# The second half of an output projection in a fixed order on the matrix engine, with router products between the halves of its tiles

## The chip, the cores and the metric

The kernel runs on one core of a Trainium2 chip. The time is the device time of one execution, in microseconds (us). A core has five engines that work side by side, each through a program of its own in order, and wait for one another by semaphores: TensorE (PE; its weight loads are shown apart, as PEld), VectorE (DVE), ScalarE (ACT), GpSimd (POOL) and SyncE (SP). Here SP issues nearly all DMA transfers, in the order of its program; POOL issues the gathers and scatters by index.

## The reference, cut to what matters

The kernel computes one layer of a decoder for 512 prompt rows and 32 sample rows: attention and a state-space mixer, an output projection, and a mixture of 16 experts. The part that changes stands between the mixers and the experts:

```
mixed = concat([rmsnorm(att), y_ssm]) @ w_out        # 1024 x 1024
x = x + mods[2] * mixed
h = rmsnorm(x, g_norm2) * (1 + mods[4]) + mods[3]
lg = h @ w_rg + b_rg ;  le = h @ w_re + b_re         # router: 4 + 16 logits
# best of 4 groups, best 2 of its 4 experts, softmax weights
y = x + mods[5] * sum over the chosen experts of weight * expert(h)
```

An expert computes `silu(h @ w_gate) * (h @ w_up)` and multiplies it by `w_down`.

## The kernel before, in words

The 512 prompt rows are four tiles of 128 rows, t = 0 to 3; the 32 sample rows are a small fifth tile. The 1024 output columns of the projection are computed in two halves of 512. Each half sums over eight blocks k of 128 inputs, taken in the order 4 to 7, then 0 to 3 (`ko`). A float32 product is made of three reduced products, since weights and inputs are each split in a high and a low part: `catH` and `catL` hold the inputs, `wH` and `wL` the weights of the second half. A tile of the second half is thus 8 x 3 = 24 products of 128x512 into one accumulator `acc`.

Every tile then goes through these steps, each of them a function before:

- `first_half(t)`: ScalarE squares the first 512 columns of `x1` and sums them; TensorE turns (transposes) these columns in four pieces into a tile of PSUM, `evac` copies them to SBUF (`h2T`) on VectorE or ScalarE by a fixed pattern, and four small products with the folded router weights `wrP` give the first part of the 20 logits (`pr`), which VectorE copies to `lg`. GpSimd multiplies the first half of the normalised row, `h2`. Of `h2` there are two buffers, so tile t+2 needs that tile t has been written out.
- `mixed_tile(t)`: the 24 products; VectorE multiplies them by the gate and adds them to `x1`.
- `routed_tile(t)`: the same squares, turns and router products for the second 512 columns; on VectorE a reciprocal root by three Newton steps (`rsqrt_col`, single-column operations), the logits, the rest of `h2`, and `rank`, six small VectorE operations that end in `Ab`, the marks of the chosen experts. SP stores `x1` to the output `y_prompt` and `h2` to `h2d` in DRAM.
- `sample_rows()`: the like for the 32 sample rows (`h2S`, `lgS`).

`Ab` of all five tiles is counted on TensorE, VectorE works out each row's place (`posm`, `oh`, `gir`), and GpSimd gathers the first expert's rows from `h2d` (`xg`, L1921). It waits for the places and for all writes to `h2d`. The experts start with these rows.

The string `OSEQ` gives the order in which the steps are written down; a planner with costs and priorities sets each engine's order from it. The router steps are written at a higher priority (`high_priority(offset=100)`), `rank` at a lower one. SP also loads expert weights here. Weight tiles `gu` share a ring of seven buffers with `wL`: the second part of expert 2 and the first part of expert 3 go to the buffers of `wL` and are loaded once the last product with it is done. The weights `gux` of expert 4 go where the sample rows' tiles stood.

`in_turn` (which stands in the program and is used for an earlier projection) ties TensorE's instructions to the order in which they are written.

Of the kernel before, what the change touches and what calls it, by code (L numbers as in the profile page):

```python
# [29 lines left out]
OSEQ = 'm0 s f0 m1 r0 f1 m2 r1 f2 f3 m3 r2 r3'  # L30
# [20 lines left out]
def hybrid_step(ctx: ExitStack, tc: tile.TileContext, a, o):  # L51
# [1555 lines left out]
    def router(src, n, w, hf):  # L1607

        with tc.high_priority(offset=100):
            pt = PS()  # L1610
            for i in range(4):
                T.transpose(pt[:, n * i:n * i + n], src[:, (4 * hf + i) * P:(4 * hf + i + 1) * P], ident[0:n, 0:n])
            hT = W(p6, [P, 4, n], F32, "h2T", 3)
            evac(hT, pt[:, 0:4 * n].rearrange("p (k c) -> p k c", c=n))
            pr = PS("pr")
            for i in range(4):
                mm(pr[0:n, 0:20], hT[:, i, :], w[:, 4 * hf + i, :], start=i == 0, stop=i == 3)
            return pr[0:n, 0:20]
# [36 lines left out]
    def sample_rows():  # L1655
        h2 = W(p6s, [NS, D], F32, "h2S", 1)
        ss = W(p6, [NS, 1], F32, "ss2")
        S.activation(h2, xs1, AF.Square, accum_out=ss)
        x = W(p6, [NS, 1], F32, "ms2")
        V.tensor_scalar(x, ss, 1.0 / D, EPS, op0=OP.mult, op1=OP.add)  # L1660
        r = rsqrt_col(x, "h2s")
        V.scalar_tensor_tensor(h2, xs1, r, a2S, op0=OP.mult, op1=OP.mult)
        V.tensor_add(h2, h2, m3S)
        SP.dma_start(h2d[512:512 + NS, :], h2)
        lgS = lg[0:NS, 4, :]
        V.tensor_tensor(lgS, router(h2, NS, wr, 0), rb[0:NS], op=OP.add)
        V.tensor_tensor(lgS, router(h2, NS, wr, 1), lgS, op=OP.add)
        rank(4)
# [36 lines left out]
    def first_half(t):  # L1705

        ss = W(p6, [P, 1], F32, "ss2")
        square(x1[:, t, :], P, 0, ss)
        V.tensor_scalar(ms[:, t:t + 1], ss, 1.0 / D, EPS, op0=OP.mult, op1=OP.add)
        V.tensor_copy(lg[:, t, :], router(x1[:, t, :], P, wrP, 0))  # L1710
        h2s[t] = W(p6, [P, D], F32, "h2")
        G.tensor_mul(h2s[t][:, 0:512], x1[:, t, 0:512], M[:, 2, 0:512])

    def mixed_tile(t):

        acc = PS("acc")
        sl = slice(t * P, (t + 1) * P)
        for k in ko:
            mm(acc, catH[:, k, sl], wH[:, k, :], start=k == ko[0], stop=False)
            mm(acc, catH[:, k, sl], wL[k // 4][:, k % 4, :], start=False, stop=False)  # L1720
            mm(acc, catL[:, k, sl], wH[:, k, :], start=False, stop=k == ko[-1])
        tmp = W(p6, [P, 512], F32, "t512", 2)
        V.tensor_tensor(tmp, acc, M[:, 0, 512:D], op=OP.mult)
        V.tensor_add(x1[:, t, 512:D], x1[:, t, 512:D], tmp)

    def routed_tile(t):
# [5 lines left out]
        r = rsqrt_col(x, "h2")  # L1732
        V.tensor_tensor(lg[:, t, :], router(xr, P, wrP, 1), lg[:, t, :], op=OP.add)
# [15 lines left out]

    for step in OSEQ.split():  # L1750
        if step == "s":
            sample_rows()
            close_p6s()
            pw2["s"], close_pws = pool("pws", "right")
            early("s")
        else:
            (first_half if step[0] == "f" else mixed_tile if step[0] == "m" else routed_tile)(int(step[1]))
            if step == "m3":
                close_p6w()
                pw2["w"], close_pww = pool("pww", "right")  # L1760
                load_part(2, 2, 1)
                load_part(3, 3, 0)
                early("w")
# [374 lines left out]
    close_pws()  # L2138
# [37 lines left out]
```

## Time and profile before

| | us |
|---|---|
| median of 3 runs | 785.82 |
| the runs | 785.45, 785.82, 791.01 |
| the profiled execution, its own time | 787.62 |
| its span, first to last instruction | 785.9 |
| PE busy | 709.3 (90%) |
| DVE busy | 501.2 (64%) |
| ACT busy | 355.2 (45%) |
| POOL busy | 151.6 (19%) |

The mean granted TensorE clock of the profiled execution was 0.938 of full speed. The span is shorter than the time by 1.7 us, which lie around it. Busy shares are means over stages with different limits; the stage of the change is the stretch from 527 us, where the products of the second half start, to 572 us, where the first gather starts. In the profile TensorE's rows are pipelined: a product that starts every 0.23 us is shown with 0.39 us of its own.

### The profile page before, as it was taken

To read this page: it belongs to the slowest core of one execution; us is meant where nothing else is said; L and a number is where in the kernel's file an instruction comes from. 1 tells how busy PE (TensorE), PEld (TensorE's weight loads), DVE (VectorE), ACT (ScalarE), POOL (GpSimd) and SP (SyncE) were. 2 spreads that over 40 slices of the span, in tenths; PEclk is the share of its full clock that TensorE was granted. 3 is DMA by queue.
4 is the path that set the end of the run, shared out by engine and by line. 5 is a ranking of instruction groups with operands and counts; after the bars stand their busy time and mean duration, and the time that the engine had idled before them with its cause. 6 is when DMAs were issued, how large, how long until landed. Compare 5 with 4: busy or idle time off the path is not lost. (4 is left out here: it accounts for less than half of the span.)

```text
span 785.9 us, 14689 instructions
## 1 busy us (share of the span) xinstructions
PE 709.3 (90%) x5565; PEld 511.7 (65%) x5565; DVE 501.2 (64%) x1333; ACT 355.2 (45%) x813; POOL 151.6 (19%) x169
## 2 busy tenths in 40 slices
PE   4999999898999578998989999899668999999993
PEld 3667877676777355665647756687655766767562
DVE  5633692524644767554557555878986888877773
ACT  3423444515233333364434435613433766677661
POOL 1103012121321421010111200020131232233221
PEclk9999999889899879699999889999868999999997
DMA  8964895144559634423445041988767899997311
GB/s 286 355 187 131 289 330 193 58 162 161 214 191 346 253 143 172 149 81 134 164 158 219 2 108 23 360 267 286 290 253 282 270 333 335 334 329 256 86 25 23
DMA packets 67094, 161.86 MB, mean 206 GB/s; under 512 B 19005, under 2 KB 31238, under 8 KB 60622
## 3 DMA queue, kind: packets, MB, share of 16 engines
q1 hardware_dynamic: 56798, 115.54, 42.3%
q0 software_dynamic: 10224, 45.37, 17.5%
q8 instruction: 44, 0.72, 0.4%
q14 instruction: 28, 0.23, 0.1%
HBM read 153.48 MB, written 20.74 MB: 222 GB/s over the span
## 5 line engine op out<-in xcount | busy, mean ns | idle before, releaser
L92 PE MATMUL acc<-wh,hH 128*128 128x512 f32 (+1 forms) x128 | 48.9, 382 | 0.5 <-issue 0.5
L92 PE MATMUL acc<-wl,hH 128*128 128x512 f32 (+1 forms) x128 | 47.3, 370 | 0.0
L92 PE MATMUL acc<-wh,hL 128*128 128x512 f32 (+1 forms) x128 | 47.1, 368 | 0.0
L817 ACT ACTIVATE psb<-s,amx 128x128 f32<-128x128 f32 (+3 forms) x64 | 33.7, 528 | 27.4 <-DVE amx L815 24.3
L92 PE MATMUL acc<-gu,XF 128*128 128x512 f32 x88 | 46.1, 606 | 0.0
L92 PE MATMUL acc<-wh,XH 128*128 128x512 f32 x68 | 44.7, 657 | 0.4 <-ACT XH L1942 0.4
L815 DVE TENSOR_REDUCE amx<-s 128x1 f32<-128x128 f32 (+3 forms) x64 | 30.9, 484 | 17.3 <-PE s L92 17.3
L92 PE MATMUL ps<-wada,scT 128*32 128x128 f32 x768 | 38.0, 301 | 4.1 <-DMA wada<-in_w_ada 3.0
L92 PE MATMUL s<-KT,QT 128*128 128x384 f32 (+3 forms) x128 | 39.3, 392 | 1.3 <-DVE qa L838 0.8
L335 DVE TENSOR_TENSOR wl<-dn,wh 128x512 fp32r<-128x512 f32 x52 | 34.0, 686 | 7.0 <-ACT wh L334 6.9
L92 PEld LDWEIGHTS ps<-wada,scT 128*32 128x32 f32 x768 | 30.6, 122 | 10.3 <-issue 3.6
L1047 POOL DMA_INDIRECT gsel<-in_cache_sel,idx x16 | 20.6, 1289 | 84.3 <-PE smo L92 72.6
L334 ACT CAST wh<-dn 128x512 fp32r<-128x512 f32 x52 | 30.9, 619 | 12.9 <-PE acc L92 11.2
L820 PE MATMUL pt<-ident,psb 128*128 128x128 f32 x160 | 33.3, 308 | 3.3 <-ACT psb L817 3.3
L1991 POOL DMA_INDIRECT out_y_prompt<-yo,gi x13 | 21.4, 1646 | 74.8 <-DVE yo L1985 20.1
L335 DVE TENSOR_TENSOR wl<-gu,wh 128x512 fp32r<-128x512 f32 x44 | 29.5, 685 | 8.4 <-ACT wh L334 7.6
L92 PE MATMUL acc<-wh,HH 128*128 128x512 f32 x68 | 32.3, 478 | 1.6 <-ACT HH L1974 1.2
L334 ACT CAST wh<-gu 128x512 fp32r<-128x512 f32 x44 | 26.1, 619 | 15.8 <-PE acc L92 10.8
L92 PE MATMUL smo<-kt,Qb 128*32 128x512 f32 x80 | 29.6, 614 | 2.3 <-DVE kt L100 2.3
L102 ACT COPY kt<-sm 128x512 f32<-128x512 f32 x32 | 18.5, 584 | 27.6 <-PE sm L1023 24.0
L1985 DVE TENSOR_TENSOR yo<-acc,M 128x512 f32<-128x512 f32 x34 | 23.1, 686 | 11.5 <-PE acc L92 9.1
L92 PE MATMUL acc<-wl,HH 128*128 128x512 f32 x68 | 28.6, 421 | 0.0
(788 smaller groups left out, 1902.9 us busy)
## 6 DMA issues: line engine op xcount, KB each, us to landing
wada<-in_w_ada SPq DMA_DIRECT2D x24, 1024.0 KB
dn<-in_w_down SPq DMA_DIRECT2D x12, 1024.0 KB
gu<-in_w_gate SPq DMA_DIRECT2D x21, 512.0 KB
gu<-in_w_up SPq DMA_DIRECT2D x21, 512.0 KB
gux<-in_w_gate SPq DMA_DIRECT2D x11, 512.0 KB
gux<-in_w_up SPq DMA_DIRECT2D x11, 512.0 KB
wt<-in_cache_win SPq DMA_DIRECT2D x4, 1024.0 KB
wout<-in_w_out SPq DMA_DIRECT2D x4, 1024.0 KB
```

The lines of the kernel that those rows point to most:

```text
L92: T.matmul(out, lhsT, rhs, start=start, stop=stop)
L102: S.copy(out, in_)
L334: S.copy(wh[:, 0:n], w)
L335: (eng or V).tensor_sub(wl[:, 0:n], w, wh[:, 0:n].bitcast(F32))
L815: V.tensor_reduce(mx, ps[:, 0:n], axis=AX.X, op=OP.max, negate=True)
L817: S.activation(pb[:, 0:n], ps[:, 0:n], AF.Exp, bias=mx, accum_out=sm[:, h:h + 1])
L820: T.transpose(pt[:, c * P:(c + 1) * P], pb[:, c * P:(c + 1) * P], ident)
L1047: G.indirect_dma_start(out=t.rearrange("p r c -> p (r c)"), out_offset=None, in_=sel_rows, in_offset=bass.IndirectOffsetOnAxis(ap=idx[:, 2 ...
L1985: V.tensor_tensor(yo[:, cols], po, M5[:, cols], op=OP.mult)
L1991: G.indirect_dma_start(out=y_p, out_offset=bass.IndirectOffsetOnAxis(ap=gi, axis=0), in_=yo, in_offset=None, bounds_check=511, oob_is_err= ...
```

## The change

The order of the steps is written anew, finer, and TensorE's instructions are tied to it by `in_turn`, step by step:

- the 24 products of a tile are cut in two halves of 12 (`a`, k = 4 to 7, and `b`, k = 0 to 3);
- `first_half` and `routed_tile` are each cut in the turns (`F`, `R`) and the router products (`f`, `r`), as are the sample rows (`S`, `s`; before them stands `s` alone, the part without TensorE);
- between the halves, and between one tile and the next, stand turns and router products: those of the first columns of the same tile, and those of the second columns of the tile before;
- the loads of weights that need freed buffers (`load_part(2, 2, 1)`, `load_part(3, 3, 0)`) are written after all steps, and those of expert 4 (`early("s")`) after the sample rows' last router product.

No arithmetic is added or left out. `rsqrt_col` gets a buffer for each tile.

```
-OSEQ = 'm0 s f0 m1 r0 f1 m2 r1 f2 f3 m3 r2 r3'
+OSEQ = 's a0 F0 b0 f0 a1 F1 b1 f1 R0 a2 r0 F2 S0 b2 f2 s0 R1 a3 r1 S1 F3 b3 f3 s1 R2 R3 r2 r3'
...
-    def router(src, n, w, hf):
-
-        with tc.high_priority(offset=100):
-            pt = PS()
...
+    def turned(src, n, hf):
+
+        pt = PS()
+        for i in range(4):
+            T.transpose(pt[:, n * i:n * i + n], src[:, (4 * hf + i) * P:(4 * hf + i + 1) * P], ident[0:n, 0:n])
+        hT = W(p6, [P, 4, n], F32, "h2T", 3)
+        evac(hT, pt[:, 0:4 * n].rearrange("p (k c) -> p k c", c=n))
+        return hT
+
+    def routed(hT, n, w, hf):
+
+        pr = PS("pr")
+        for i in range(4):
+            mm(pr[0:n, 0:20], hT[:, i, :], w[:, 4 * hf + i, :], start=i == 0, stop=i == 3)
+        return pr[0:n, 0:20]
...
+    def first_turn(t):
         ss = W(p6, [P, 1], F32, "ss2")
         square(x1[:, t, :], P, 0, ss)
         V.tensor_scalar(ms[:, t:t + 1], ss, 1.0 / D, EPS, op0=OP.mult, op1=OP.add)
-        V.tensor_copy(lg[:, t, :], router(x1[:, t, :], P, wrP, 0))
+        hT["f", t] = turned(x1[:, t, :], P, 0)
+
+    def first_route(t):
+        V.tensor_copy(lg[:, t, :], routed(hT["f", t], P, wrP, 0))
...
+    def sample_turn(hf):
+        hT["s", hf] = turned(hS[0], NS, hf)
+
+    def sample_route(hf):
+        V.tensor_tensor(lgS, routed(hT["s", hf], NS, wr, hf), lgS if hf else rb[0:NS], op=OP.add)
+        if hf:
+            rank(4)
+            close_p6s()
+            pw2["s"], pw2["close_s"] = pool("pws", "right")
+            early("s")
+
+
+    steps = dict(F=first_turn, f=first_route, R=second_turn, r=second_route, S=sample_turn, s=sample_route)
     for step in OSEQ.split():
         if step == "s":
-            sample_rows()
-            close_p6s()
-            pw2["s"], close_pws = pool("pws", "right")
-            early("s")
+            sample_start()
+        elif step[0] in "ab":
+            t = int(step[1])
+            in_turn(mixed, t, ko[0:4] if step[0] == "a" else ko[4:8])
+            if step[0] == "b":
+                mixed_end(t)
         else:
-            (first_half if step[0] == "f" else mixed_tile if step[0] == "m" else routed_tile)(int(step[1]))
-            if step == "m3":
-                close_p6w()
-                pw2["w"], close_pww = pool("pww", "right")
-                load_part(2, 2, 1)
-                load_part(3, 3, 0)
-                early("w")
+            in_turn(steps[step[0]], int(step[1]))
+    close_p6w()
+    pw2["w"], close_pww = pool("pww", "right")
+    load_part(2, 2, 1)
+    load_part(3, 3, 0)
+    early("w")
```

The first place is TensorE's program around the last tile. Before, this is what stands behind tile 3's last product (`acc_6281`): the sample rows' router products, then turns (`ps`, L1612) and router products (`pr`) of the prompt tiles.

```order
-L92 MATMUL acc_6281<-wH,catL_5516 128x512
-L92 MATMUL pr_6031<-wr_5660,h2T_6029 32x20 x2
-L92 MATMUL pr_6044<-wr_5660,h2T_6042 32x20
-L92 MATMUL pr_6031<-wr_5660,h2T_6029 32x20
-L92 MATMUL pr_6044<-wr_5660,h2T_6042 32x20
-L92 MATMUL pr_6031<-wr_5660,h2T_6029 32x20
-L92 MATMUL pr_6044<-wr_5660,h2T_6042 32x20 x2
-L1612 MATMUL ps_6071<-ident,x_5501 128x128 x4
-L1612 MATMUL ps_6129<-ident,x_5501 128x128 x4
-L1612 MATMUL ps_6159<-ident,x_5501 128x128 x4
-L92 MATMUL pr_6078<-wrP_5689,h2T_6076 128x20 x4
```

All eight turns and eight router products of the prompt tiles stand behind the last product. Now, from tile 3's last product (`acc_6213`) to the end of the steps:

```order
+L92 MATMUL acc_6213<-wH,catL_5516 128x512
+L92 MATMUL pr_6278<-wrP_5689,h2T_6261 128x20 x4
+L92 MATMUL pr_6286<-wr_5660,h2T_6250 32x20 x4
+L1611 MATMUL ps_6324<-ident,x_5501 128x128 x4
+L1611 MATMUL ps_6346<-ident,x_5501 128x128 x4
+L92 MATMUL pr_6353<-wrP_5689,h2T_6329 128x20 x4
+L92 MATMUL pr_6372<-wrP_5689,h2T_6351 128x20 x4
```

Two turns and three router products of prompt tiles are left behind the last product, with one of the sample rows; six turns, five router products of prompt tiles and one of the sample rows now stand in front of it.

The second place is the end of VectorE's program in this stage, tile 3's normalised rows (`h_1322`), the end of tile 2's ranking (first `Ab` row) and the whole ranking of tile 3, as it stands now:

```order
+L1750 SCALAR_TENSOR_TENSOR lg<-lg,rsq_zh_3_1338_6338,rbP_5687 128x20
+L1759 SCALAR_TENSOR_TENSOR h_1322_6284<-h_1322_6284,rsq_zh_3_1338_6338,M 128x512 x2
+L1655 SCALAR_TENSOR_TENSOR Ab<-rk,og 128x16
+L1648 TENSOR_TENSOR rkb_6380<-lg 128x20x4
+L1649 TENSOR_TENSOR rkb_6380<-lg 128x20x4
+L1651 TENSOR_TENSOR rkb_6380<-rkb_6380,msk_5697 128x160
+L1653 TENSOR_REDUCE rk<-rkb_6380 128x20
+L1654 TENSOR_SCALAR og<-rk 128x4
+L1655 SCALAR_TENSOR_TENSOR Ab<-rk,og 128x16
```

Both halves of tile 3's `h2` stand in front of the ranking of tile 3, and of the last operation of tile 2's ranking. The rankings of tiles 0 and 1 (but for the last two operations of tile 1) have moved in front of the multiplication of tile 3's `acc`.

The third place is SP's program, from the third store of `y_prompt` on, as it stands now (`gu_6396` is the second part of expert 2, `gu_6399` the first part of expert 3, `gux` expert 4):

```order
+L1751 DMA out_y_prompt<-x_5501 128x1024
+L1573 DMA gu_6396<-in_w_gate 128x1024
+L1573 DMA gu_6396<-in_w_up 128x1024
+L1573 DMA gux_6303<-in_w_gate 128x1024
+L1573 DMA gux_6303<-in_w_up 128x1024
+L1573 DMA gux_6306<-in_w_gate 128x1024
+L1763 DMA h2d<-h_1283_6088 128x1024
+L1573 DMA gux_6306<-in_w_up 128x1024
+L1573 DMA gu_6399<-in_w_gate 128x1024
+L1573 DMA gu_6399<-in_w_up 128x1024
+L1751 DMA out_y_prompt<-x_5501 128x1024
+L1763 DMA h2d<-h_1302_6183 128x1024
```

The store `h2d<-h_1283` is tile 1's. Five loads of 0.5 MB now stand in front of it and behind the third store of `y_prompt`; before, the four loads of `gux` stood behind the second store of `y_prompt`, and `gu` (2, 1) behind tile 0's `h2d`.

## Rows read from the trace of the kernel before

**Rows 1.** The page's first line.

```profile
span 785.9 us, 14689 instructions
```

**Rows 2.** Stretches: us from:to, length, busy PE, PEld, DVE, ACT, POOL (instructions), clock, DMA, GB/s.

```profile
527.00:550.40 23.40, 23.40 (x120) 18.49 (x108) 20.79 (x52) 7.57 (x22) 4.70 (x2) 1.00 0.86 302
550.40:562.80 12.40, 11.82 (x119) 11.22 (x118) 11.34 (x51) 6.53 (x11) 1.88 (x1) 1.00 0.94 367
562.80:572.00 9.20, 1.38 (x31) 0.99 (x26) 8.37 (x36) 4.62 (x8) 1.26 (x1) 0.50 0.31 119
```

**Rows 3.** Timeline of PE: start, length, engine, line, what, [idle before].

```profile
550.12 0.39 PE L92 MATMUL acc<-wL,catH 128*128 128x512 f32 x1
550.35 0.39 PE L92 MATMUL acc<-wH,catL 128*128 128x512 f32 x1
550.67 0.68 PE L92 MATMUL pr<-wr,h2T 128*32 128x20 f32 x16
...
554.83 1.86 PE L92 MATMUL pr<-wrP,h2T 128*128 128x20 f32 x16
556.53 0.64 PE L1612 MATMUL ps<-ident,x 128*128 128x128 f32 x4
557.00 0.97 PE L92 MATMUL pr<-wrP,h2T 128*128 128x20 f32 x8
```

**Rows 4.** Timeline of DVE, behind the last product.

```profile
550.78 0.69 DVE L1723 TENSOR_TENSOR t<-acc,M 128x512 f32<-128x512 f32 x1
...
552.41 0.69 DVE L100 COPY h2T<-ps 128x512 f32<-128x512 f32 x1 [0.75 <-PE ps L1612]
553.02 0.68 DVE L1724 TENSOR_TENSOR x<-x,t 128x512 f32<-128x512 f32 x1
553.62 0.16 DVE L1667 TENSOR_TENSOR lg<-pr,lg 32x20 f32<-32x20 f32 x1
...
555.95 0.85 DVE L1651 TENSOR_SCALAR og<-rk 32x4 f32<-32x4 f32 x1
...
563.34 1.19 DVE L1652 SCALAR_TENSOR_TENSOR Ab<-rk,og 128x16 bf16<-128x16 f32 x1
...
568.70 0.17 DVE L1652 SCALAR_TENSOR_TENSOR Ab<-rk,og 128x16 bf16<-128x16 f32 x1
```

**Rows 5.** Groups by shape, 527 to 572 us: count, busy us, mean ns, idle before.

```profile
L1648 DVE TENSOR_TENSOR rkb<-rkb,msk 128x160 f32<-128x160 f32 x4 | 1.3, 316 | 0.0
L1650 DVE TENSOR_REDUCE rk<-rkb 128x20 f32<-128x160 f32 x4 | 1.3, 314 | 0.0
L1645 DVE TENSOR_TENSOR rkb<-lg 128x80 f32<-128x80 f32 x4 | 0.9, 231 | 0.0
L1734 DVE SCALAR_TENSOR_TENSOR lg<-lg,rsq_zh,rbP 128x20 f32<-128x20 f32 x4 | 0.9, 229 | 0.0
L1710 DVE COPY lg<-pr 128x20 f32<-128x20 f32 x4 | 0.7, 174 | 0.3 <-PE pr L92 0.3
```

**Rows 6.** Timeline of POOL.

```profile
554.90 1.88 POOL L1712 TENSOR_TENSOR h<-x,M 128x512 f32<-128x512 f32 x1 [23.20 <-DMA h2d<-h]
563.23 1.26 POOL L1712 TENSOR_TENSOR h<-x,M 128x512 f32<-128x512 f32 x1 [6.45 <-DVE lg L1734]
572.02 1.39 POOL L1921 DMA_INDIRECT xg<-h2d,gir  x1 [7.52 <-DVE gm L1813]
```

**Rows 7.** Timeline of SP: issues of DMA.

```profile
546.86 0.38 SPq L1747 DMA_DIRECT2D h2d<-h  x1
...
552.08 0.33 SPq L1747 DMA_DIRECT2D h2d<-h  x1
...
562.30 0.32 SPq L1747 DMA_DIRECT2D h2d<-h  x1
567.16 1.05 SPq L1745 DMA_DIRECT2D h2d<-h  x2
```

**Rows 8.** Stretch of the experts' start, columns as in Rows 2.

```profile
602.00:606.00 4.00, 3.64 (x13) 2.60 (x11) 2.99 (x8) 0.98 (x3) 2.70 (x3) 0.50 0.46 135
```

More of the change, by code (lines that the diff above doesn't have):

```diff
@@ L1605, in hybrid_step @@
     V.tensor_tensor(wrP, wr, aT[:, :, None].to_broadcast([P, KC, 20]), op=OP.mult)
-    def router(src, n, w, hf):
-        with tc.high_priority(offset=100):
-            pt = PS()
[L1611 to L1618, printed above, removed]
+    def turned(src, n, hf):
[10 more added lines that the diff above has]
+        return pr[0:n, 0:20]
     def square(xr, n, hf, ss):
@@ L1664, in sample_rows @@
         SP.dma_start(h2d[512:512 + NS, :], h2)
[L1665 to L1668, printed above, removed]
+        return h2
     mixS = W(p6s, [NS, D], F32, "h2S", 1)
@@ L1703, in hybrid_step @@
     h2s = {}
-    def first_half(t):
+    hT = {}
+    def first_turn(t):
         ss = W(p6, [P, 1], F32, "ss2")
@@ L1709, in first_half, with mixed @@
         V.tensor_scalar(ms[:, t:t + 1], ss, 1.0 / D, EPS, op0=OP.mult, op1=OP.add)
-        V.tensor_copy(lg[:, t, :], router(x1[:, t, :], P, wrP, 0))
+        hT["f", t] = turned(x1[:, t, :], P, 0)
+    def first_route(t):
+        V.tensor_copy(lg[:, t, :], routed(hT["f", t], P, wrP, 0))
         h2s[t] = W(p6, [P, D], F32, "h2")
         G.tensor_mul(h2s[t][:, 0:512], x1[:, t, 0:512], M[:, 2, 0:512])
-    def mixed_tile(t):
-        acc = PS("acc")
+    accs = {}
+    def mixed(t, ks):
+        if t not in accs:
+            accs[t] = PS("acc")
+        acc = accs[t]
         sl = slice(t * P, (t + 1) * P)
-        for k in ko:
+        for k in ks:
             mm(acc, catH[:, k, sl], wH[:, k, :], start=k == ko[0], stop=False)
@@ L1721, in mixed_tile, with mixed_end, second_turn @@
             mm(acc, catL[:, k, sl], wH[:, k, :], start=False, stop=k == ko[-1])
+    def mixed_end(t):
         tmp = W(p6, [P, 512], F32, "t512", 2)
-        V.tensor_tensor(tmp, acc, M[:, 0, 512:D], op=OP.mult)
+        V.tensor_tensor(tmp, accs[t], M[:, 0, 512:D], op=OP.mult)
         V.tensor_add(x1[:, t, 512:D], x1[:, t, 512:D], tmp)
-    def routed_tile(t):
+    rs = {}
+    def second_turn(t):
         xr = x1[:, t, :]
@@ L1731, in routed_tile, with second_route @@
         V.tensor_scalar(x, ss, 1.0 / D, ms[:, t:t + 1], op0=OP.mult, op1=OP.add)
-        r = rsqrt_col(x, "h2")
-        V.tensor_tensor(lg[:, t, :], router(xr, P, wrP, 1), lg[:, t, :], op=OP.add)
+        rs[t] = rsqrt_col(x, f"h2_{t}")
+        hT["r", t] = turned(xr, P, 1)
+    def second_route(t):
+        xr, r = x1[:, t, :], rs[t]
+        V.tensor_tensor(lg[:, t, :], routed(hT["r", t], P, wrP, 1), lg[:, t, :], op=OP.add)
         V.scalar_tensor_tensor(lg[:, t, :], lg[:, t, :], r, rbP, op0=OP.mult, op1=OP.add)
@@ L1748, in routed_tile, with sample_start @@
             rank(t)
+    hS = [None]
+    lgS = lg[0:NS, 4, :]
+    def sample_start():
+        hS[0] = sample_rows()
+    def sample_turn(hf):
[8 more added lines that the diff above has]
+    steps = dict(F=first_turn, f=first_route, R=second_turn, r=second_route, S=sample_turn, s=sample_route)
     for step in OSEQ.split():
         if step == "s":
-            sample_rows()
-            close_p6s()
-            pw2["s"], close_pws = pool("pws", "right")
-            early("s")
-        else:
-            (first_half if step[0] == "f" else mixed_tile if step[0] == "m" else routed_tile)(int(step[1]))
-            if step == "m3":
-                close_p6w()
-                pw2["w"], close_pww = pool("pww", "right")
-                load_part(2, 2, 1)
-                load_part(3, 3, 0)
-                early("w")
+            sample_start()
[4 more added lines that the diff above has]
+                mixed_end(t)
+        else:
+            in_turn(steps[step[0]], int(step[1]))
[4 more added lines that the diff above has]
+    early("w")
     close_p6()
@@ L2137, in hybrid_step @@
     close_pww()
-    close_pws()
+    pw2["close_s"]()
     close_pwu()
```

## The prediction

> **What bounds the kernel now.** I began with the first line of the page: the span is 785.9 us [rows 1], and the profiled execution's own time is 787.62 us. The chain of waits follows only the end of the program back and does not reach the stage of the change, so I read that stage by stretches of time, then engine by engine in the timeline.
>
> The stretches [rows 2] show one stage in three parts. From 527 to 550.4 us TensorE is busy all the time at full clock with the 96 products; VectorE is busy for 20.79 of 23.40 us beside it. From 550.4 to 562.8 us TensorE still has work (11.82 us of 12.40), the turns and router products, and VectorE is nearly full too. From 562.8 to 572 us TensorE has 1.38 us of work in 9.20, while VectorE works for 8.37. So the stage ends on VectorE: behind the last product, whose multiplication starts at 550.78, it runs until the last marks `Ab` end at 568.87 [rows 4], which makes 18.1 us. The first gather starts at 572.02 [rows 6], and the experts cannot start before it.
>
> The reader should see two bounds in a row. Up to the last product it is TensorE; from there it is VectorE, which has to finish logits, ranks and normalised rows of several tiles. TensorE's work behind the last product is hidden under VectorE's. What the change moves ahead on TensorE therefore gets longer in front, and only what VectorE can do earlier is gained behind.
>
> **The change part by part.**
>
> *TensorE in front of the last product.* Six turns, five router products of prompt tiles and one of the sample rows move ahead of it. Four turning instructions take from 556.53 to 557.00, 0.47 us. Two router products take from 554.83 to 556.53, 0.85 us each. The two of the sample rows are shown with 0.68 us together, so one is put at 0.3 [rows 3]. That makes 6 x 0.47 + 5 x 0.85 + 0.3 = 7.4 us. The turns of the sample rows stood among the products already and cost nothing new. The last product ended at 550.35 + 0.39 = 550.74 [rows 3]; it will end at about 558.1. Each router product has twelve products between itself and its turn, 12 x 0.23 = 2.8 us by two starts [rows 3], against a copy of 0.69 [rows 4]; I expect no wait there, 0.5 us in all as an upper bound.
>
> *VectorE behind the last product.* Its 18.1 us lose what now stands earlier. A row's length overlaps the next by 0.08 us (0.68 long, the next starts 0.60 later [rows 4]), so I count each length less 0.08.
> - Two copies of turned rows (0.69): 1.2 us.
> - Logits of three first halves (0.17) and of tiles 0 and 1 in full (an addition like the 0.16 of [rows 4], a scaling 0.23 [rows 5]): 0.3 + 0.2 + 0.3 = 0.8 us.
> - The whole ranking of tile 0 and four of the six rows of tile 1's: two comparisons at 0.23, a mask at 0.32, a reduction at 0.31 [rows 5], and two small ones like the last `Ab`'s 0.17 [rows 4]. Less 0.08 each this is 0.95 for six and 0.77 for four: 1.7 us.
> - One half row of `h2` of tile 2, another 512-column product like the one of 0.68: 0.6 us.
> - One meeting with GpSimd. `og` took 0.85 us at 555.95 [rows 4] beside GpSimd's row of 554.90 [rows 6], against 0.17 for the small row without such company: 0.7 us. That GpSimd row, tile 2's, now falls under the products. Tile 3's (563.23 [rows 6], beside an `Ab` of 1.19 [rows 4]) stays behind them and I keep its 1.0 us.
> - The wait of 0.75 us for a turn [rows 4] goes, since the turns come early.
>
> Together 5.75 us; 12.35 us are left. What is late next is unchanged in kind: the root, the two rows of `h2` and the ranking of tile 3, all in one program on VectorE, in which tile 3's `h2` stands ahead of its ranking. Tile 3's logits need sum, turn, copy and router product, about 0.69 + 0.68 + 0.64 + 0.69 + 0.97 = 3.7 us; VectorE has as much other work there. A new wait of up to 0.8 us is possible, at the square of tile 3.
>
> The Trainium skill ("SBUF — State Buffer", Who interferes with whom) says that a VectorE instruction with two inputs in SBUF and a GpSimd instruction that reads SBUF exclude each other for the whole instruction, and that the second to issue waits in full. The row agrees: `Ab` of 1.19 us ends when GpSimd's 1.26 does. By the rule both meetings could recur wherever the GpSimd rows land; if the moved one cost VectorE the same on the path, the sum would be 0.7 us higher.
>
> *SP and the transfers.* No transfer is added. The loads for experts 2, 3 and 4 come later: the first waits for the last product of tile 3's first half with `wL`, at about 558.1 - 2.8 - 2 x 0.47 - 0.85, so near 554; the last waits for the last product. Eight loads and the stores of tiles 1 and 3, 0.52 MB each, then pass in one stretch. At 0.367 MB per us [rows 2] the 2.6 MB in front of tile 1's `h2d` store and that store take 8.6 us: it lands near 563 and GpSimd's row for tile 3 (1.26 us [rows 6]) follows. VectorE wants it near 568, since two rows of `h2` (1.3 us) and a ranking (0.95) stand between that point and the end. All 6.3 MB, with the stores of tiles 2 and 3, are through by 554.5 + 17 = 571.6, against a gather that would start at 572.02 + 1.65 = 573.7 [rows 6]. The cover is thin, 2 us; what it costs when it goes is the second rival. The experts need these weights only behind the gather, so their delay itself costs nothing.
>
> *Sum.* 7.4 - 5.75 = +1.65 us at the last `Ab`, which the gather and all experts follow. Low bound: the second meeting with GpSimd goes as well (-1.0), +0.6. High bound: 0.8 for the new wait and 0.5 for TensorE, +3.0. I take the middle of the worked terms, +1.7: 789.3 us against the profiled execution's 787.62. That execution lies 1.8 us above the median of the runs; against the median of 785.82 it is **787.5 us**. A measurement of this kernel cannot tell less than about 1% (7.9 us) from no change, so this is a forecast of no change.
>
> **The rivals.**
>
> *The tail on VectorE collapses.* If VectorE had gaps enough under the longer stretch of TensorE and only tile 3's chain were left, the end would come 3.7 us of logits, a scaling and a ranking of 1.6 and six hand-overs of 0.1 behind 558.1, at about 564: -4.9 us, 781 us. For it speaks that VectorE has 2.6 us of 23.40 free under the products and the stretch grows by 7.4. Against it: the rows of VectorE's new program put tile 2's root, sample ranking and both rows of `h2` of tiles 2 and 3 between, and they need tile 2's or tile 3's sums. 5%.
>
> *Slower: the stores wait behind the weights.* Before, tile 0's `h2d` store was issued at 546.86 [rows 7], and GpSimd's next row waited for it until 554.90 [rows 6], 8 us for 0.52 MB: stores queue behind loads. The last stores, issued at 567.16 [rows 7], had the transfers nearly to themselves (119 GB/s [rows 2]). Now more loads stand in front. The point from which this decides: tile 3's last store lands later than 573.7. At 302 GB/s [rows 2] the 6.3 MB end at 554.5 + 20.9 = 575.4, and the gather is 1.7 us later still: 789.2 us. Beyond 1% it would need under 248 GB/s over the whole stretch (at 240 it is 26.3 us, end at 580.8, 7.1 on top: 794.6 us). 12% for the first, 3% for the second. The Trainium skill ("DMA: Bandwidth & Descriptors", Queues, rings and completion order) says that a DMA engine takes the descriptors of one ring in order; by that rule no store from SP overtakes SP's loads, and the time is the one of this rival whenever the rate is low. The 8 us above agree.
>
> *The experts start in another phase.* The granted clock was half in the stretch 562.8 to 572 [rows 2] and again in 602 to 606, behind a short pause of TensorE [rows 8]. The planner also sets a few instructions of the experts in another order. If that second stretch does not come, half of its 4 us are won: 785.5 us; if one more comes, as much is lost: 789.5 us. 12% each.
>
> *The change does not do what it says.* The planner could have kept the old order; the rows of TensorE's program show that it did not. Under 1%.
>
> **How the numbers follow.** The forecast itself has 55%, with a range of its own of 786.4 to 788.8. The likeliest time is 787.5 us. For 8 in 10 the range takes the forecast's own bounds with the experts' phase on either side, 786.4 - 2.0 and 788.8 + 2.0, rounded out to 784.0 and 791.0 us; the stores at 302 GB/s lie inside, the collapse of the tail and the low rate outside. Faster by over 1% (below 778) needs more than the collapse: 2%. Slower by over 1% (above 793.7): the low rate, 4% with the rest. No change: 94%.
>
> **What would show it.** Right: the last product with `acc` ends near 558; VectorE's stretch from there to the last `Ab` is 12 to 13 us; the last `Ab` ends near 570.5 and the gather starts near 573.7, 1 to 3 us later than now; TensorE is free of waits up to 563. Wrong: the last product ends well ahead of 557 or behind 559 (the moved work has another price); the last `Ab` comes before 568 (VectorE did fill its gaps); the gather starts more than 3.5 us behind the last `Ab` (the stores are late); or the stretch from the gather to the end, 785.9 - 572.02 = 213.9 us now [rows 1, 6], changes by more than 2 us (the experts' phase).

## The result, and the profile after

The changed kernel takes **791.0 us** at the median of 15 runs (783.85 to 794.19); 15 runs of the kernel before beside them have 785.82 us (781.24 to 791.75). The ratio is **1.006, 95% interval 1.0035 to 1.0085**, about 4.7 us more. The interval leaves 1 out, so the kernel is slower, by less than the bound of 1% below which the forecast speaks of no change. The median lies 3.5 us above the predicted 787.5 and on the upper end of the range. A loss of 4.7 us where 1.7 was worked out needs an explanation, so this is what the experiments are about.

The profiled execution took 787.71 us, with a span of 786.0 [rows 1 has 785.9]. Equal spans would mislead: this execution reached the stage of the change 9.7 us sooner. The view of stretches from the start to the first product with `wH` shows why, first of the kernel before, then of the change (us from:to, length, busy PE, PEld, DVE, ACT, POOL, clock, DMA, GB/s):

```profile
0.00:527.28 527.28, 480.98 (x4459) 350.57 (x4459) 300.28 (x860) 214.16 (x541) 88.05 (x123) 0.94 0.55 189
```

```profile
0.00:517.58 517.58, 472.52 (x4459) 345.59 (x4459) 300.00 (x860) 214.23 (x541) 88.24 (x123) 0.96 0.55 193
```

The same 4459 products ran, with less of the time at the half clock. So I count every time from that product, **S**, and name the first turn of gathered rows **X** (`ps<-ident,xg`, the experts' first work on TensorE). S and X are these two points in time; "theory S" and "theory X" further down are two hypotheses and have nothing to do with them. The timeline of TensorE before, and then of the change (start, length, engine, line, what, [idle before]):

```profile
527.28 0.50 PE L92 MATMUL acc<-wH,catH 128*128 128x512 f32 x1
...
576.87 1.09 PE L1938 MATMUL ps<-ident,xg 128*128 128x128 f32 x4 [1.91 <-DMA xg<-h2d,gir]
```

```profile
517.58 0.50 PE L92 MATMUL acc<-wH,catH 128*128 128x512 f32 x1
...
548.19 0.39 PE L92 MATMUL acc<-wH,catL 128*128 128x512 f32 x1
...
572.06 1.12 PE L1974 MATMUL ps<-ident,xg 128*128 128x128 f32 x4 [1.69 <-DMA xg<-h2d,gir]
```

S to X was 49.59 us and is 54.48: **+4.9 us**, the size of the measured loss. The stretches of the change, which answer to [rows 2]:

```profile
517.58:548.59 31.01, 31.01 (x183) 26.24 (x179) 26.09 (x72) 9.72 (x26) 5.70 (x3) 1.00 0.65 231
548.59:553.30 4.71, 4.50 (x49) 3.97 (x49) 4.36 (x27) 2.64 (x5) 0.00 (x0) 1.00 0.99 247
553.30:564.27 10.97, 0.42 (x11) 0.28 (x8) 7.72 (x26) 4.38 (x6) 1.70 (x1) 0.57 0.92 365
564.27:567.43 3.16, 0.73 (x16) 0.56 (x15) 2.39 (x14) 1.78 (x4) 0.00 (x1) 0.50 0.06 21
```

TensorE is busy without a gap for 31.0 us, against 23.46 before: +7.5, where 7.4 was worked out. But VectorE, which should now be full from there to the last `Ab`, works for 7.72 us of 10.97 in the third line, while the transfers are busy at 0.92. Its timeline, which answers to [rows 4], names the wait:

```profile
555.28 0.24 DVE L1649 TENSOR_TENSOR rkb<-lg 128x80 f32<-128x80 f32 x1
558.64 0.69 DVE L1756 TENSOR_TENSOR h<-x,M 128x512 f32<-128x512 f32 x1 [3.12 <-DMA h2d<-h]
...
559.37 1.26 DVE L1651 TENSOR_TENSOR rkb<-rkb,msk 128x160 f32<-128x160 f32 x1
...
564.10 0.17 DVE L1655 SCALAR_TENSOR_TENSOR Ab<-rk,og 128x16 bf16<-128x16 f32 x1
```

At 558.64 VectorE writes the second half of tile 3's `h2` and has waited 3.12 us for the store that still reads that buffer, tile 1's. The 1.26 us behind it is a meeting with GpSimd, whose own row for tile 3 waited for the same store. From the last product to the last `Ab` it is 564.27 - 548.59 = 15.7 us, not 12.35. The timeline of GpSimd [rows 6]:

```profile
539.09 1.28 POOL L1716 TENSOR_TENSOR h<-x,M 128x512 f32<-128x512 f32 x1 [17.08 <-DMA h2d<-h]
558.75 1.70 POOL L1716 TENSOR_TENSOR h<-x,M 128x512 f32<-128x512 f32 x1 [18.38 <-DMA h2d<-h]
567.43 1.40 POOL L1957 DMA_INDIRECT xg<-h2d,gir  x1 [6.98 <-DVE gm L1849]
```

And the issues on SP [rows 7], where tile 1's store is the row of 546.56:

```profile
536.35 0.33 SPq L1763 DMA_DIRECT2D h2d<-h  x1
...
543.84 0.34 SPq L1573 DMA_DIRECT2D gu<-in_w_gate  x1
544.23 0.42 SPq L1573 DMA_DIRECT2D gu<-in_w_up  x1
544.70 0.43 SPq L1573 DMA_DIRECT2D gux<-in_w_gate  x1
545.17 0.64 SPq L1573 DMA_DIRECT2D gux<-in_w_up  x1
545.92 0.54 SPq L1573 DMA_DIRECT2D gux<-in_w_gate  x1
546.56 0.61 SPq L1763 DMA_DIRECT2D h2d<-h  x1
547.22 0.75 SPq L1573 DMA_DIRECT2D gux<-in_w_up  x1
```

Tile 0's store (536.35) had the transfers to itself and was done by 539.09, 2.7 us later. Tile 1's store stands behind five loads of 0.52 MB and was done 12 us later. In the kernel before, the four `gux` loads stand much further ahead, at S + 14.6 to 19.1 instead of S + 27.1 to 29.6:

```profile
541.91 0.46 SPq L1573 DMA_DIRECT2D gux<-in_w_gate  x1
542.41 1.43 SPq L1573 DMA_DIRECT2D gux<-in_w_up  x1
545.95 0.33 SPq L1573 DMA_DIRECT2D gux<-in_w_gate  x1
546.33 0.43 SPq L1573 DMA_DIRECT2D gux<-in_w_up  x1
```

From X to the end it is 213.9 us, against 209.0 before. In this execution VectorE waited 4.67 us for a scatter at 678.47 (2.23 us before, at 680.73) and TensorE 2.26 us behind it. Whether that belongs to the change is the first question to the chip.

### The profile page after: what moved, and what is told of

The parts are those of the page before. It is cut to its first block, busy times and chain, and to the rows that moved or that the text cites. A ratio compares the mean times of both kernels' runs of the same rounds, so it can differ in the third digit from the quotient of the medians.

```text
span 786.0 us, 14696 instructions
## 1 busy us (share of the span) xinstructions
PE 703.3 (89%) x5565; PEld 508.1 (65%) x5565; DVE 501.8 (64%) x1333; ACT 355.5 (45%) x813; POOL 149.4 (19%) x169
## 5 line engine op out<-in xcount | busy, mean ns | idle before, releaser
L92 PE MATMUL s<-KT,QT 128*128 128x384 f32 (+3 forms) x128 | 37.2, 373 | 1.3 <-DVE qa L838 0.8
L335 DVE TENSOR_TENSOR wl<-gu,wh 128x512 fp32r<-128x512 f32 x44 | 29.6, 688 | 9.5 <-ACT wh L334 8.8
L92 PE MATMUL acc<-wl,XH 128*128 128x512 f32 x68 | 28.8, 423 | 2.3 <-DVE wl L335 2.3
L92 PE MATMUL acc<-wl,HH 128*128 128x512 f32 x68 | 29.6, 436 | 0.0
```

The source lines that it names most:

```text
L92: T.matmul(out, lhsT, rhs, start=start, stop=stop)
L335: (eng or V).tensor_sub(wl[:, 0:n], w, wh[:, 0:n].bitcast(F32))
```

## The experiments

Theory **S**: VectorE's wait for tile 1's store costs the difference between forecast and result. Out of its failure came theory **Q**: the loads that the change lets go late share the transfers with whatever stands beside them, first tile 1's store, then the last stores, then the gathered rows. The rivals are in the expectations. All times in us; "gather" is the start of the first gather. Each ratio is to the kernel before on the same chip. The runs of one kernel scatter by 5 to 12 us, mostly with the mean granted clock: over the 224 runs that are compared, each taken against the mean of its own kernel, 0.01 of clock goes with 6.0 us, and with that taken out their standard deviation falls from 2.8 to 1.3 us. The last column is the difference to the runs of before by that line at equal clock, with 1.96 standard errors; it is my working, the ratio is the measurement. The column is rough: a kernel also has a hand in its own clock (S to X ran at 0.86 on the mean before, at 0.84 and 0.82 in the two profiles of the change), and that part is taken out with the rest.

| kernel | last `Ab` - S | gather - S | X - S | X to end | ratio (95%) | at equal clock |
|---|---|---|---|---|---|---|
| before | 41.59 | 44.74 | 49.59 | 209.0 | 1 | 0 |
| the change | 46.69 | 49.85 | 54.48 | 213.9 | 1.006 (1.0035-1.0085) | |
| e0_again | 46.69 | 49.84 | 54.48 | 209.7 | 1.0058 (1.0015-1.0101) | +4.1 ± 1.0 |
| e1_own_rows | 42.19 | 49.53 | 54.31 | 212.4 | 1.0083 (1.0048-1.0118) | +4.8 ± 1.2 |
| e2_store_first | 42.26 | 49.20 | 53.89 | 213.4 | 1.0080 (1.0041-1.0119) | +4.5 ± 1.4 |
| e3_more_indices | 46.71 | 49.86 | 54.54 | 209.6 | 1.0047 (1.0010-1.0083) | +3.7 ± 1.0 |
| e4_loads_last | 42.19 | 45.34 | 55.12 | 209.0 | 1.0063 (1.0029-1.0096) | +3.9 ± 0.6 |
| e5_products_first | 45.31 | 48.47 | 53.21 | 211.0 | 1.0053 (1.0021-1.0086) | +3.1 ± 0.8 |
| e6_two_tiles_ahead | 39.85 | 43.00 | 52.32 | 211.3 | 1.0057 (1.0022-1.0092) | +6.2 ± 1.0 |
| e7_one_tile_ahead | 43.31 | 46.47 | 56.13 | 210.5 | 1.0073 (1.0036-1.0111) | +4.2 ± 0.9 |
| e10_loads_after_gather | 42.20 | 45.34 | 50.00 | 221.8 | 1.0137 (1.0088-1.0186) | +11.5 ± 1.1 |
| e9_two_tiles_loads_after | 39.87 | 43.01 | 47.66 | 218.8 | 1.0093 (1.0062-1.0124) | +7.7 ± 0.8 |
| eb_before_loads_after | 43.89 | 47.03 | 51.88 | 219.8 | 1.0131 (1.0089-1.0174) | +9.4 ± 1.1 |
| e12_sample_early | 42.96 | 46.11 | 50.86 | 209.0 | 1.0049 (1.0021-1.0078) | +1.8 ± 0.9 |

**The change once more, unaltered.**

> The changed kernel once more, unaltered, for a second profile. Counted in every run from TensorE's first product with wH: to the last Ab it took 41.6 us before and 46.7 us in the first profile of the change; from the first gather to the end 213.9 and 218.6 us. Theory S (the store): the stage of the change itself is longer, so 46.7 again within 0.7, with VectorE waiting about 3 us for tile 1's h2d store. Theory X (the experts' rows stand in another order): VectorE's wait of 4.67 us for a scatter and TensorE's 2.26 us behind it come again at the same row, gather to end 218 to 219 us. Theory C (chance of the clock): that wait does not come again or TensorE loses nothing by it, and gather to end is 214 +- 1 us. Time by S alone: 1.004 to 1.007 of before; by S and X together 1.010 to 1.012.

The stage repeats to 0.01 us, with 3.00 us of waiting in place of 3.12. X to end is 209.7, as before the change. VectorE's wait for the scatter came again, 3.33 us at 684.77, but TensorE lost only 0.92 us behind it instead of 2.26, and the 4 us of the first profile did not come again. Of these, 1.4 us were lost in the first 31 us behind X, the rest from the 2.26 us on, behind which the granted clock stood at half from 681.2 to 684.6. So theory X, in which the loss comes with the wait, falls; chance stays, and the loss to explain is the 4.9 us from S to X.

**The wait taken away, in two ways.** In one, tile 3's `h2` has its own place; in the other the store goes first.

```diff
-        h2s[t] = W(p6, [P, D], F32, "h2")
+        h2s[t] = W(p6, [P, D], F32, "h2") if t < 3 else M[:, 0, :]
```

> Tile 3's h2 gets a place of its own (the rows of M that the out-projection has done with), so that neither GpSimd nor VectorE waits for tile 1's h2d store. Theory S: VectorE's wait of 3.1 us goes, from the end of the last product with acc to the last Ab 12.0 to 13.0 us instead of 15.7, first product with wH to last Ab 43 to 44 us, and the time falls by about 3 us against the change (ratio to before 1.001 to 1.003). Rival R (VectorE is bound there by its own work and by meetings with GpSimd): the wait is replaced by other idle time or longer rows, stage 45.5 us or more, time as the change's.

```diff
+            store[t] = SP.dma_start(h2d[t * P:(t + 1) * P, :], h2).ins
...
+    with tc.issue_after(store[1]):
         load_part(2, 2, 1)
         load_part(3, 3, 0)
         early("w")
```

(`early("s")` in the sample steps is put behind it in the same way.)

> The two h2 buffers stay; the loads for experts 2, 3 and 4 that the change put ahead of tile 1's h2d store on SP are issued behind it. Theory S with the queue as its cause: the store is issued about 1 us behind VectorE's last row of tile 1 and lands 2 to 4 us later instead of 12, tile 3's rows wait for nothing, stage 43 to 44 us, time about 3 us under the change's. Rival B (the store is slow because the transfers as a whole are full, not because of what stands ahead of it): it lands 8 us or more after its issue, VectorE still waits, time as the change's.

What S says of the wait is right: VectorE's stretch falls to 11.2 us in both, and in the second the store issued at 545.42 let GpSimd's next row start at 548.54, 3.1 us later. Ahead of the loads the store was done in 3.1 us; behind five of them the same store took 12. But S is wrong on the time: X comes only 0.2 and 0.6 us sooner, and the runs are no faster. The gather starts 7 us behind the last `Ab` instead of 3.2. In the first of the two, VectorE had the places ready (`gir`, 563.30), and the stretch from the issue of the last stores (558.95) to the gather shows what it waited for; timelines of SP, VectorE and GpSimd, then the stretch:

```profile
558.95 0.98 SPq L1761 DMA_DIRECT2D h2d<-M  x2
```

```profile
563.30 0.16 DVE L1914 TENSOR_SCALAR gir<-rt 128x1 int32<-128x1 f32 x1 [0.52 <-PE rt L92]
```

```profile
568.43 1.48 POOL L1957 DMA_INDIRECT xg<-h2d,gir  x1 [26.75 <-ACT wh L334]
```

```profile
558.95:568.43 9.48, 1.85 (x41) 1.54 (x40) 6.80 (x28) 0.79 (x2) 0.00 (x0) 0.50 0.62 240
```

The releaser named in GpSimd's row had long been done. The transfers moved 240 GB/s over this stretch, and the last packet of SP's queue ended at 567.21, 1.2 us ahead of the gather; in the second run it was 565.63 and 566.84, 1.2 us again. With VectorE's wait gone, the last stores are late next, behind the same loads.

**More index tiles for the experts.** Six buffers instead of four (`PS("rt"), "2", 6, e`).

> The index tiles of the experts' gathers and scatters get six buffers instead of four, so that VectorE no longer waits for a scatter to be done before it writes the next indices; the stage of the change stays as it is (46.7 us). Theory X: the wait of 4.67 us goes, TensorE's 2.26 us and the half clock behind it (3.4 us at half speed, 1.7 us) go with it, gather to end 214 to 215 us, and the time falls by about 4 us against the change. Theory C: gather to end as in the repeated change, time the same within 1.5 us. The planner orders the experts' rows anew for it, which by itself may move that stretch by 1 to 2 us either way.

The wait for the scatter is gone, and X to end is 209.6, like the repeated change's 209.7. The wait of 3.33 us there cost nothing that shows in the time.

**The loads behind the last store.**

```diff
-            early("s")
...
+    with tc.issue_after(store[3]):
         load_part(2, 2, 1)
+        early("s")
         load_part(3, 3, 0)
```

> The change with its order of products, but the eight loads for experts 2, 3 and 4 are issued behind the last h2d store instead of ahead of tile 1's. Counted from TensorE's first product with wH, the first gather starts at 44.7 us before the change, at 49.9 with it, and at 49.5 and 49.2 in the two runs in which only VectorE's wait was taken away: there the last Ab came at 42.2 and the gather 7 us later. Theory Q (the last stores queue behind 4 MB of weights): now the last Ab comes at 42.2 again, the gather 3.2 us later at 45.4 +- 0.5, and the time is 4 to 4.5 us under the change's, ratio to before 1.000 to 1.002. Rival W (the weights then come too late): the eight loads end about 14 us after the last store, and if an expert waits for them, gather to end is over 217 us instead of 214 and the gain is lost there. Rival G (the gather waits for something else than the stores): it stays at 49.

Ab and gather come as theory Q says, at 42.2 and 45.3. Yet X comes 9.8 us behind the gather instead of 4.7, and the gain is gone before the experts begin. Timeline of TensorE, then the stretch from the first of the loads:

```profile
580.91 1.12 PE L1976 MATMUL ps<-ident,xg 128*128 128x128 f32 x4 [4.82 <-DMA xg<-h2d,gir]
```

```profile
567.00:581.00 14.00, 2.35 (x52) 1.97 (x52) 12.62 (x47) 3.21 (x8) 6.16 (x8) 0.50 1.02 325
```

The transfers are full, and the gathered rows come 5 us late beside the loads. The view of the queues tells more; the first row is SP's queue from 573 to 575 us, the others are the queue of GpSimd's gathers from 575 to 577, 577 to 579 and 579 to 581 (packets, MB, share of the 16 engines):

```profile
q1 hardware_dynamic: 135, 0.52, 102.3%
...
q0 software_dynamic: 24, 0.10, 13.0%
...
q0 software_dynamic: 83, 0.31, 37.6%
...
q0 software_dynamic: 112, 0.43, 51.9%
```

For comparison, the gathers' queue in the kernel before, where no load stood beside it, from 574 to 576 us; its first gather was issued at 572.02:

```profile
q0 software_dynamic: 119, 0.48, 86.4%
```

There the first packet moved 2.1 us after the start of the issue (574.1); here, with the gather issued at 571.13, it moved 4.7 us after it (575.8), and only from 579 on had the gather half of the engines. So about 2.6 us of the delay of 5 lie ahead of its first packet and the rest in the slower packets. The Trainium skill ("DMA: Bandwidth & Descriptors", Queues, rings and completion order) says that a DMA engine serves the queues that have work in turn, packet by packet. The last row of the first view, with 51.9%, agrees; why the first packet came later is not shown. None of the rivals had named this cost.

**Other orders.** One with the products in one piece, and two with fewer router products ahead of the last product.

```diff
-OSEQ = 's a0 F0 b0 f0 a1 F1 b1 f1 R0 a2 r0 F2 S0 b2 f2 s0 R1 a3 r1 S1 F3 b3 f3 s1 R2 R3 r2 r3'
+OSEQ = 's a0 b0 a1 b1 a2 b2 S0 S1 a3 b3 s0 s1 F0 R0 F1 f0 R1 r0 F2 f1 F3 r1 f2 R2 f3 R3 r2 r3'     # e5
+OSEQ = 's a0 F0 b0 f0 a1 R0 b1 r0 F1 a2 f1 R1 b2 r1 a3 b3 S0 S1 F2 s0 F3 s1 f2 R2 f3 R3 r2 r3'     # e6, loads as in e4
+OSEQ = 's a0 F0 b0 f0 a1 b1 R0 a2 r0 b2 S0 S1 a3 b3 s0 s1 F1 R1 F2 f1 F3 r1 f2 R2 f3 R3 r2 r3'     # e7, loads as in e4
```

> The split steps and the fixed order of the change, but with the 96 products in one piece as before and nearly all turns and router products behind them; the loads are left where the pools free them. If the place of the router products is what costs (both the 7.5 us of TensorE and the late loads), everything is as before: TensorE 23.5 to 24 us, VectorE 17.5 to 18.5 us behind it, gather at 44.2 to 45.5 us from the first product, ratio 0.998 to 1.002. If the fixed order as such costs (a turn that has to wait for its neighbour), TensorE idles among the router products and the gather comes at 47 us or later.

> Only the router products of tiles 0 and 1 stand among the products, those of the sample rows and of tiles 2 and 3's first halves behind the last product, where VectorE has other work; loads behind the last store. TensorE's stretch is 23.5 + 4 turns at 0.47 + 4 router products at 0.85 = 28.7 us; if VectorE's stretch of 11.2 us grows by the copies and logits that come late (1 to 1.5 us), the gather is at 28.7 + 12.5 + 3.2 = 44.4 us, 0.3 us ahead of the kernel before and 1 us ahead of the run with all of them in front: ratio 0.999. If VectorE's stretch grows by all that the front loses (2.3 us and more), the gather is at 45.4 us or later and nothing is won.

> Only tile 0's two router products stand among the products, everything else behind the last; loads behind the last store. TensorE's stretch 23.5 + 2 x 1.32 = 26.1 us. If VectorE had gaps under the products before (2.6 us of 23.4) that tile 0's logits and ranking fill, its stretch falls from 18.1 by 3 us or more and the gather is at 44.0 us or earlier, 0.7 us ahead of the kernel before. If what TensorE does earlier only replaces what VectorE does later, one for one, the gather is at 44.7 +- 0.5 us and the time is that of before, ratio 0.998 to 1.002.

e5 is inconclusive, and its gather, at 48.5, missed the expected 44.2 to 45.5. TensorE's stretch is 23.45 us as before, but VectorE's is 21.9 instead of 18.1: written down behind the products, the steps' VectorE work also moved behind them (it idled 4.98 us before tile 3's `acc`). A turn that waits for its neighbour was not the reason: TensorE idled 0.74 us among its router products. The string orders more than TensorE. e6 has its gather at 43.0, 1.4 us ahead of its own expectation, and e7's at 46.5, later than expected; in both the loads behind the last store take that back, 9.3 and 9.7 us from gather to X. At equal clock e6 stands at +6.2 though its X comes 2.2 us ahead of the change's; that difference I cannot explain.

**The loads behind the gathers.** `LATE` names the loads that wait for the second gather:

```diff
-LATE = ((3, 2), (5, 0))
+LATE = ((2, 1), (4, 0), (4, 1), (3, 0), (3, 2), (5, 0))
```

(and the calls that issued them earlier go; on the change's order, on e6's, and on the kernel before.)

> The change with its order of products; the eight loads for experts 2, 3 and 4 are issued behind the first two gathers of the experts instead of in front of tile 1's h2d store. Let S be TensorE's first product with wH and X its first turn of gathered rows. S to X took 49.6 us before, 54.5 in both profiles of the change, 54.3 and 53.9 where only VectorE's wait was gone (the last stores landed late), and 55.1 where the loads stood right behind the last store: there the gather started at 45.4, but X came 9.8 us behind it instead of 4.7. Theory Q (the loads share the transfers with the stores or with the gathered rows, whichever they stand beside): last Ab at 42.2, gather at 45.4, X at 50.1 +- 0.5, and the time falls by 4 us against the change, ratio 0.999 to 1.002. Rival W (the experts then run out of weights): X to end, 209.0 us before and 209 to 214 in the profiles since, grows by 4 us or more and the ratio stays at 1.005. Rival G (the gathered rows come late for another reason): X at 54 us or later again.

> The order with the router products of tiles 0 and 1 alone among the products, where the gather started at 43.0 us from S but X came only at 52.3; now with the eight loads behind the first two gathers. Theory Q: gather at 43.0, X at 47.7 +- 0.5 us, 1.9 us ahead of the kernel before, and if the experts take as long as before the ratio is 0.997 to 0.999: the first version ahead of both. Rival W (weights late): X at 47.7 all the same, but X to end grows by as much as X came earlier or more, 211 to 215 us, ratio 1.002 to 1.006.

> The kernel before, with its own order of products and only the eight loads moved behind the first two gathers. By theory Q nothing in the stage waited for them there: last Ab at 41.6 us from S, gather at 44.7, X at 49.6 as before. What it adds is the price of late weights by itself: if the experts have enough of them in stock, X to end stays at 209 +- 1.5 us and the ratio is 0.998 to 1.002; if they run out (rival W), X to end grows by 4 us or more, up to the 11 us by which the loads come later, ratio 1.005 to 1.013, and then no version that holds them back can win.

S to X does what Q says in the first two: 50.0 and 47.7 us, the second 1.9 us ahead of the kernel before. In the third the last `Ab` came 2.3 us later than expected: VectorE waited for router products there, up to 1.42 us. Behind X the gain is gone in all three: X to end grows to 219 to 222 us. Rival W (the experts then run out of weights) forecasts such a growth, in the second of 215 at most. But that weights come late is not shown to be the cause. Stretches of 100 us from X and of the 30 us behind them, first of the kernel before, then of the kernel before with late loads:

```profile
576.87:676.87 100.00, 95.42 (x462) 65.82 (x463) 80.00 (x194) 58.59 (x112) 22.50 (x16) 0.93 0.91 316
676.87:706.87 30.00, 30.00 (x126) 20.60 (x125) 23.20 (x46) 20.18 (x39) 9.44 (x8) 1.00 0.95 324
```

```profile
577.87:677.87 100.00, 94.05 (x457) 65.10 (x457) 77.33 (x188) 55.93 (x107) 20.72 (x16) 0.93 0.99 353
677.87:707.87 30.00, 25.77 (x98) 16.83 (x94) 20.68 (x39) 17.82 (x33) 5.47 (x4) 0.94 0.78 254
```

In the first 100 us the transfers are fuller, 0.99 against 0.91, but TensorE works only 1.4 us less. Most is lost in the next 30 us, 98 instructions against 126, and there the transfers have room again (0.78). By then the loads had caught up: the one that SP issues 71.8 us behind X in the kernel before (648.67) is issued 71.8 us behind X with late loads too (649.69). TensorE's waits for other engines in those 30 us are short, the longest 1.85 us. What also differs is the order of the experts' work that the planner made for it: of the 841 instructions of TensorE behind X, 484 have the same tiles at the same place. Whether the late weights or this other order costs the 10 us stays open; no run held that order fixed.

**The loads let go in time.** What put them late in the change is the place of the sample rows' steps: `early("s")` is written in the last of them. One edit of the change's order puts these steps back behind tile 1:

```diff
-OSEQ = 's a0 F0 b0 f0 a1 F1 b1 f1 R0 a2 r0 F2 S0 b2 f2 s0 R1 a3 r1 S1 F3 b3 f3 s1 R2 R3 r2 r3'
+OSEQ = 's a0 F0 b0 f0 a1 F1 b1 f1 S0 S1 R0 a2 r0 s0 s1 F2 b2 f2 R1 a3 r1 F3 b3 f3 R2 R3 r2 r3'
```

> The change with one edit of its order: the turns and router products of the sample rows stand behind tile 1's products again (before its change of place they ended at about S + 15; in the change at S + 31), so that the space of the sample rows comes free and expert 4's four loads can start at about S + 15 instead of S + 27 to 30. TensorE's stretch stays 31.0 us. Theory Q with its cause (the loads were let go late, and everything behind them in the transfers, tile 1's store, the last stores, the gathered rows, came late): VectorE does not wait for tile 1's store, last Ab at 42.2 to 42.7, gather at 45.4 to 45.9, first turn of gathered rows at 50.0 to 50.6 against 54.5 with the change and 49.6 before, to the end 209 to 211 us; ratio to before 1.000 to 1.003. Rival K (the order of the products itself costs the time, through TensorE's 7.5 us): first turn at 53.5 us or later, ratio 1.005 or more. Rival L (the two loads that wait for the last products are enough to hold up the stores): gather 5 us or more behind the last Ab.

The four `gux` loads go at S + 13.6 to 16.0 (S is 525.26 here), tile 1's store follows only two loads, and VectorE no longer waits for it. Rows of SP, GpSimd, and TensorE at X:

```profile
538.88 0.41 SPq L1573 DMA_DIRECT2D gux<-in_w_gate  x1
539.34 0.45 SPq L1573 DMA_DIRECT2D gux<-in_w_up  x1
540.58 0.68 SPq L1573 DMA_DIRECT2D gux<-in_w_gate  x1
541.30 0.43 SPq L1573 DMA_DIRECT2D gux<-in_w_up  x1
...
552.21 0.33 SPq L1573 DMA_DIRECT2D gu<-in_w_gate  x1
552.59 0.42 SPq L1573 DMA_DIRECT2D gu<-in_w_up  x1
555.45 0.33 SPq L1763 DMA_DIRECT2D h2d<-h  x1
```

```profile
558.51 1.49 POOL L1716 TENSOR_TENSOR h<-x,M 128x512 f32<-128x512 f32 x1 [5.22 <-DMA h2d<-h]
571.37 1.39 POOL L1957 DMA_INDIRECT xg<-h2d,gir  x1 [11.37 <-DVE gm L1849]
```

```profile
576.12 1.09 PE L1974 MATMUL ps<-ident,xg 128*128 128x128 f32 x4 [1.81 <-DMA xg<-h2d,gir]
```

X is at 50.86, 3.6 us sooner than with the change and 1.27 behind the kernel before; the gather is 3.15 us behind the last `Ab`, so rival L (the two loads suffice to hold up the stores) falls, and X to end is 209.0. TensorE still has its 31.2 us, so rival K (the order of the products itself costs the time) falls for the stage: it wanted X at 53.5 or later. At equal clock +1.8 ± 0.9 us is left of +4.1. The ratio missed the expected 1.000 to 1.003: 1.0049, with 1.0021 as its lower end, does not tell this kernel from the change's 1.0058. The statement rests on the stage and, more weakly, on the equal clock. X is 0.26 us behind the expected span of 50.0 to 50.6, and last `Ab` and gather miss theirs by about as much. Now tile 0's store stands behind the four `gux` loads: issued at 544.23, it let VectorE go on at 551.47, after a wait of 1.47 us, all of it ahead of the last product. No version ran ahead of the kernel before: the only one with an earlier X lost 10 us behind it.

## Why the prediction was right and where it failed

- **The bound and TensorE's price: right.** Last product at S + 31.0 against 23.46: +7.54, worked out as 7.4. TensorE waits for nothing in front, and its wait for VectorE's marks later costs nothing.
- **VectorE's own work: right in kind, 1.1 us too careful.** Without the wait it needs 11.2 us from the last product, not 12.35: it lost 6.9 us, not 5.75. The meeting with GpSimd that I kept, 1.0 us, can go too. With the wait, as the change stands, it is 15.7 us.
- **The sum: +1.65 was the price of the two engines.** With the loads in time, the order costs 7.77 us on TensorE, less 6.40 on VectorE and 0.10 between gather and X: +1.27 us from S to X. In the change as measured the gather came 5.1 us later than before, where 1 to 3 was forecast.
- **The step that failed: "VectorE wants it near 568" and "so their delay itself costs nothing".** VectorE needed tile 1's buffer at 555.5 of the profile of the change, S + 37.9, where I had 568, S + 40.7: I looked at the scaling rows and missed the product of line 1756, which writes the same buffer and stands ahead of tile 2's last ranking rows. And the store was done at S + 41.1, not S + 35.7. I counted 3.1 MB up to and with that store at 367 GB/s, 8.6 us. From the first load to its end 14.8 us passed, and by the stretches of the change (the last two columns are the share and the rate of the transfers) 4.4 MB moved, 1.3 MB more than I counted:

```profile
543.84:546.56 2.72, 2.72 (x22) 2.43 (x21) 2.24 (x5) 0.89 (x3) 0.00 (x0) 1.00 0.60 178
546.56:550.00 3.44, 3.44 (x28) 3.01 (x27) 2.52 (x9) 0.00 (x0) 0.00 (x0) 1.00 1.05 291
550.00:554.00 4.00, 3.23 (x33) 2.69 (x31) 3.68 (x27) 3.33 (x6) 0.00 (x0) 1.00 0.94 255
554.00:558.64 4.64, 0.00 (x0) 0.00 (x0) 1.52 (x6) 2.26 (x3) 0.00 (x0) 0.60 1.03 411
```

  The mean rate was 298 GB/s, not 367, and some of what stands behind the store moved beside it: the store of `y_prompt` that stands ahead of the first load was already through. The need 2.8 us earlier and the landing 5.3 us later turned a margin of 5 us into a wait of 3.1.
- **The rival "the stores wait behind the weights" (15%) was the mechanism**, at another place than I put it: not the last store in front of the gather, but tile 1's store in front of VectorE. Where that was removed, the rival came at its own place, with the gather 7 us behind the last `Ab`.
- **The experts' phase.** From the gather to the end it was 213.9 us before and 218.5 in the first profile of the change, more than the 2 us that the prediction names as a sign of being wrong; the second profile had 214.35. Two executions of the same kernel thus differ by 4 us there, where the rival had counted 2 us for another phase of the clock; the half clock behind TensorE's 2.26 us was a part of it.
- **The chances.** No change had 94%, and it is none by the bound of 1%, though the interval is far narrower than the prediction thought a measurement could be: it tells a loss of 0.35 to 0.85% from none. The forecast's own range, 786.4 to 788.8, was missed. The wide range held the time only by its edge, 791.0, and that was luck: its last 2 us stood for the experts' phase, and the loss came from a store.

## What to carry to other kernels

When steps are moved on one engine, list which buffers they let go and which loads hang on these; a load that is let go 12 us later stands in front of other transfers, and what it delays may be in a third engine's program. When a wait is taken away and the time does not move, measure to the point where the stages meet (here X), since the next in the queue (here the last stores, then the gathered rows) takes its place. Look there whether the order of what follows has changed as well: with the loads behind the gathers the planner also ordered the experts anew, and the two effects could not be told apart. Runs that differ by their clock are compared from a common instruction on, not by their spans.

## What the runs showed of the hardware

- The stage repeats to 0.02 us from run to run (46.69, 46.69, 46.71 us to the last `Ab`) while the time of the whole program scatters by 5 to 12 us, most of it with the mean granted clock: 6.0 us for 0.01, and the two levels in the rows are full and half speed.
- A store of 0.52 MB was done 2.7 us after its issue with free transfers, 3.1 us after it with loads only behind it, and 12 us after it behind five loads and beside three that came later.
- A gather from GpSimd's queue was held up by loads on SP's queue: its rows were turned 9.8 us after the start of its issue instead of 4.6 to 4.9, its first packet moved after 4.7 us instead of 2.1, and it had half of the engines only 8 us on.
